# Where two norms' column sums, five transposes and one unread product stand in a matrix engine's stream

## The chip, the cores and the metric

The kernel runs on 1 core of one Trainium2 chip. The metric is the device time in microseconds (us) of that core, the median of the runs shown. TensorE (PE) multiplies, VectorE (DVE), ScalarE (ACT) and GpSimd (POOL) work element by element, SyncE (SP) and GpSimd issue DMAs.

## What is computed

One layer of a hybrid decoder for 256 prompt tokens and 8 x 4 sample tokens with the same weights: an SSD branch and a gated linear attention branch, merged by gates, then cross-attention into 256 memory tokens, then a causal ConvFFN, with an RMS norm ahead of each. Cut to the part that the change touches:

```python
def _rmsnorm(x, g):
    x32 = x.astype(jnp.float32)
    y = x32 * lax.rsqrt(jnp.mean(x32 * x32, axis=-1, keepdims=True) + EPS)
    return (y * g.astype(jnp.float32)).astype(x.dtype)
...
    h = h + _cross_attend(_rmsnorm(h, p['norm_cross']), mem_k, mem_v, p['w_cq'], p['w_co'])

    up = _rmsnorm(h, p['norm_ffn']) @ p['w_up']
    up, ffn_conv_new = _causal_dwconv(up, ffn_conv, p['ffn_conv_w'], p['ffn_conv_b'])
    a, gt = jnp.split(up, 2, axis=-1)
    h = h + (jax.nn.silu(gt) * a) @ p['w_down']
```

D_MODEL is 2048, the ConvFFN is 5632 wide, all data are float32.

## The kernel before

Features lie on the 128 partitions and the 288 tokens (256 + 32) along the free axis, so a projection is `weights^T x activations` with 288 columns. Every projection goes through `proj_w`. It takes two blocks of 128 output columns at a time (a **column pair**, two PSUM accumulators, `j` = 0 and 1) and walks over the input rows in steps of two blocks of 128 (`k`). A weight block is loaded by SP, rounded by ACT to a high part (`whi`, line 103), and DVE takes the remainder as the low part (`wlo`, line 105); five buffers of each let that run ahead of PE. For each step and each `j`, PE does **a six**: four products with the high weights (lines 147 and 148: high and low part of the activations, for two `k`), then two with the low weights (line 151). A column pair over 2048 input rows has 8 steps, so 16 sixes. Sixes, back to back, are most of the program.

The list `late` holds small jobs that are to go into the stream: `proj_w` runs it (`flush`, line 155) behind the third step of a column pair. `tc.block(schedule_with_timeline_sim=True)` lets a scheduler order each engine's instructions by a simulated timeline when the program is built; `tc.keep_in_program_order` pins an instruction against that. What order comes out is shown below from the built program.

Three things in the stretch from the cross-attention to the ConvFFN matter here:

- **The norm's sum.** While the residual `h` is made, its squares are added up in `sqa`. `rstd_of` (line 1394) multiplies `sqa` by a matrix of ones (line 1396, one product of 288 columns in plain float32, where the sixes use the rounded format), which sums over the partitions; ACT then makes the reciprocal root (lines 225 and 226). This is done once for the cross-attention norm (called when the first column pair of `w_cq` is finished, in `q_proj`) and once for the ConvFFN norm (when the first column pair of `w_up` is finished, in `ffn_conv`). The norm is applied to the products' results, so the sixes don't wait for it.
- **The ConvFFN vectors.** Its convolution weights come as rows (`frow`) by DMA and are turned by five transposes on PE (line 1673, `ffn_cols`) into columns `fcol`, between two sixes of the sixth of the eight column pairs of `w_co` (`wo[5]`).
- **The nudge.** `nudge` (lines 119 to 125) puts two transposes of the identity, which nobody reads, behind the third step of the next column pair after the ConvFFN norm's sum.

From there the ConvFFN runs 44 blocks of `w_up` (two halves each) and the products with `w_down`, in sixes alone, to the end of the program.

Of the kernel before, what the change touches and what calls it, by code (L numbers as in the profile page):

```python
# [16 lines left out]
P = 128  # L17
# [6 lines left out]
T = SEQ + NS  # L24
# [18 lines left out]
def hybrid_step(ctx: ExitStack, tc: tile.TileContext, I: dict, O: list):  # L43
# [4 lines left out]
    MM, TR = nc.tensor.matmul, nc.tensor.transpose  # L48
# [12 lines left out]
    def acc_tiles(n):  # L61

        turn[0] += 1
        return [ps.tile([P, 512], F32, tag=f"acc{turn[0] % 2}", bufs=2, name="acc") for _ in range(n)]

    def mm_tile():
        return ps.tile([P, 512], F32, tag="mm", bufs=3, name="mm")

    def la_tile():
        return ps.tile([P, 512], F32, tag="la", bufs=1, name="la")  # L70


    ident = const.tile([P, P], F32, name="ident")
    make_identity(nc, ident)
    ones = const.tile([P, P], F32, name="ones")
# [24 lines left out]
    def wsplit(raw):  # L100

        hi = wp.tile(list(raw.shape), F32R, tag="whi", bufs=WB, name="whi")
        S.copy(hi, raw)  # L103
        lo = wp.tile(list(raw.shape), F32R, tag="wlo", bufs=WB, name="wlo")
        V.tensor_tensor(lo, raw, hi, ALU.subtract)  # L105
        return hi, lo
# [8 lines left out]
        return raw  # L115

    late = []

    def nudge(n):

        def f():
            a = la_tile()
            for _ in range(2):
                tc.keep_in_program_order(TR(a[0:n, 0:P], ident[:, 0:n], ident))
        late.append(f)

    def flush():

        while late:
            late.pop(0)()  # L130

    def proj_w(load, ncol, X, nk, cons, N=T):

        nt = (ncol + P - 1) // P
        accs = acc_tiles(nt)
        for k0 in range(0, nk, 4):
            kn = min(4, nk - k0)
            raw = load(k0, kn)
            for s0 in range(0, kn, 2):
                hi, lo = wsplit(raw[:, s0:s0 + 2, :])  # L140
                for j in range(nt):
                    m = min(P, ncol - j * P)
                    a = accs[j][0:m, 0:N]
                    cs = slice(j * P, j * P + m)
                    for k in range(2):
                        xh, xl = X(k0 + s0 + k)
                        MM(a, hi[:, k, cs], xh, start=(k0 + s0 + k == 0), stop=False)  # L147
                        MM(a, hi[:, k, cs], xl, start=False, stop=False)  # L148
                    for k in range(2):
                        xh, xl = X(k0 + s0 + k)  # L150
                        MM(a, lo[:, k, cs], xh, start=False, stop=(k0 + s0 + k == nk - 1))  # L151
                    if k0 + s0 + 2 == nk:
                        cons(j, a)
                if k0 + s0 == min(4, nk - 2):
                    flush()
                yield
# [7 lines left out]
    def proj(w, c0, ncol, X, nk, cons, row0=0):  # L164
        def load(k0, kn):
            return wload(rows_of(w, row0, k0, kn, c0, ncol))
        return proj_w(load, ncol, X, nk, cons)

    def run(*gens):
        for g in gens:  # L170
            for _ in g:
                pass
# [20 lines left out]
    def split(hi, lo, src):  # L193
        S.copy(hi, src)
        V.tensor_tensor(lo, src, hi, ALU.subtract)
# [27 lines left out]
    def rstd_from(pl, ssq, n, four=False):  # L223
        r = pl.tile([P, T], F32, tag="rstd", bufs=1, name="rstd")
        S.activation(r, ssq, ACT.Ln, scale=1.0 / n, bias=epsc[:, 1:2] if four else epsc[:, 0:1])
        S.activation(r, r, ACT.Exp, scale=-0.5)
        return r
# [1165 lines left out]

    def rstd_of():
        ssq = mm_tile()
        MM(ssq[:, 0:T], ones, rst.pop(), start=True, stop=True)
        return rstd_from(pb, ssq[:, 0:T], D)

    rst = []
    hn = halves(bigr, "hn")  # L1400
    acc = pb.tile([P, T], F32, tag="sqa", bufs=1, name="sqa")
    for j2 in range(KT // 2):
        def cons(j, a, j2=j2):
            added(hx[j2][:, j, :], 2 * j2 + j, a, vec("norm_cross"), hn, acc)
# [18 lines left out]
    def q2(name):  # L1423
        return px.tile([P, 2, 256], F32R, tag="q2", bufs=4, name=name)
# [51 lines left out]
    rc = []  # L1476

    def q_proj(hd):

        qp = []  # L1480
        qps.append(qp)
        for j2 in range(2):
            def cons(j, a, j2=j2):
                if not rc:
                    rc.append(rstd_of())
                if j == 0:
                    qp.append((q2("qh"), q2("ql")))
                d = 2 * j2 + j
                qs = px.tile([P, SEQ], F32, tag="qs", bufs=1, name="qs")
                V.tensor_tensor(qs, a[:, 0:SEQ], rc[0][:, 0:SEQ], ALU.mult)  # L1490
                split(qp[j2][0][:, j, :], qp[j2][1][:, j, :], qs)
                V.tensor_tensor(qsm[:, d], a[:, SEQ:T], rc[0][:, SEQ:T], ALU.mult)
            yield from proj(I["w_cq"], 512 * hd + 256 * j2, 256, hn, KT, cons)
# [126 lines left out]
    def out_cons(j2):  # L1620
        return lambda j, a: added(res["h"][:, 2 * j2 + j, :], 2 * j2 + j, a, vec("norm_ffn"), res["hf"], res["acc"])

    wo = [proj(I["w_co"], 256 * j2, 256, co, KT, out_cons(j2)) for j2 in range(KT // 2)]
    weave(q_proj(0), first_keys(), 16, 16)
    for hd in range(4):
        main = q_proj(hd + 1) if hd < 3 else chain(steps(wo[0], 6), steps(wo[1], 6))
        weave(main, attend(hd), 16 if hd < 3 else 12, 22 if hd else 18)
# [5 lines left out]
    fcol = pf.tile([P, 4, 88], F32, name="fcol")  # L1633
# [43 lines left out]
                V.tensor_copy(gfin, a[:, 0:KT])  # L1677
        carried_turn(0)

    run(*wo[:5])  # L1680
    late.append(ffn_cols)
    run(*wo[5:])
    rst.append(acc)
    rf = []
    store = []

    def ffn_conv(ct, a, out, st, cache):
        if not rf:
            rf.append(rstd_of())
            nudge(P)  # L1690
        u = pf.tile([P, SEQ], F32, tag="fu", bufs=3, name="fu")
        sp = pf.tile([P, NB, 6], F32, tag="fsp", bufs=4, name="fsp")
        G.tensor_copy(sp[:, :, 0:2], st.rearrange("p (b k) -> p b k", k=2))  # L1693
        V.tensor_tensor(u, a[:, 0:SEQ], rf[0][:, 0:SEQ], ALU.mult)
        V.tensor_tensor(sp[:, :, 2:6], a[:, SEQ:T].rearrange("p (b l) -> p b l", l=NL),
                        rf[0][:, SEQ:T].rearrange("p (b l) -> p b l", l=NL), ALU.mult)
        w2, wb = fcol[:, 2, ct:ct + 1], fcol[:, 3, ct:ct + 1]
        S.activation(out[:, 0:SEQ], u, ACT.Identity, scale=w2, bias=wb)
        S.copy(cache[:, 0:2], u[:, SEQ - 2:SEQ])
        S.copy(cache[:, 2:18].rearrange("p (b k) -> p b k", k=2), sp[:, :, 4:6])  # L1700
        outs = out[:, SEQ:T].rearrange("p (b l) -> p b l", l=NL)
        V.tensor_scalar(outs, sp[:, :, 2:6], w2, wb, ALU.mult, ALU.add)
        for k in range(2):
            s = 2 - k
            V.scalar_tensor_tensor(outs, sp[:, :, k:k + 4], fcol[:, k, ct:ct + 1], outs, ALU.mult, ALU.add)  # L1705
            V.scalar_tensor_tensor(out[:, s:SEQ], u[:, 0:SEQ - s], fcol[:, k, ct:ct + 1], out[:, s:SEQ], ALU.mult, ALU.add)
# [17 lines left out]
    def ffn_up(b0, n):  # L1724
        pr = bigr2("pr")
        nb = (b0 + BLK - 1) // BLK
        fst = fsts[nb]
        carried_load(nb + 2)
        carried_turn(nb + 1)
        c = cin[(b0 + BLK - 1) // BLK % 2]  # L1730
        for q0 in range(b0, b0 + n, 4):
            for j2 in range(2):
                av = [pf.tile([P, T], F32, tag="av", bufs=4, name="av") for _ in range(2)]

                def consa(j, a, j2=j2, av=av):
                    t = 2 * j2 + j
                    ffn_conv(q0 + t, a, av[j], fst[:, q0 - b0 + t, 0, :], c[:, 0, q0 - b0 + t, 0:18])

                def consg(j, a, j2=j2, av=av):
                    t = 2 * j2 + j  # L1740
                    gv = pf.tile([P, T], F32, tag="gv", bufs=3, name="gv")
                    ffn_conv(FT + q0 + t, a, gv, fst[:, q0 - b0 + t, 1, :], c[:, 1, q0 - b0 + t, 0:18])
                    S.activation(gv, gv, ACT.Silu)
                    V.tensor_tensor(gv, gv, av[j], ALU.mult)
                    kk = q0 - b0 + t
                    split(pr[:, kk, :], pr[:, BLK + kk, :], gv)
                c0 = (q0 + 2 * j2) * P
                run(proj(I["w_up"], c0, 256, hf, KT, consa))
                run(proj(I["w_up"], FF + c0, 256, hf, KT, consg))
        store.append((b0, n, c))  # L1750
        return pr
# [77 lines left out]
    a = acc_tiles(1)[0]  # L1829
# [62 lines left out]
```

## Time and profile before

| what | us |
| --- | --- |
| three runs | 2503.89, 2500.59, 2503.36 (median 2503.36) |
| the profiled execution, its own time | 2501.66 |
| its span in the trace | 2499.9 |
| PE busy | 2481.9 (99% of the span) |

The span is the time from the first to the last instruction in the trace. Matrix products are pipelined: a product's time in a row runs from its start to its modelled end and overlaps the next one's, so the pace of a stream is read from the starts, or from how many products lie in a stretch, and not from the mean duration.

### The profile page before, as it was taken

To read this page: it belongs to the slowest core of one execution; us is meant where nothing else is said; L and a number is where in the kernel's file an instruction comes from. 1 tells how busy PE (TensorE), PEld (TensorE's weight loads), DVE (VectorE), ACT (ScalarE), POOL (GpSimd) and SP (SyncE) were. 2 spreads that over 40 slices of the span, in tenths; PEclk is the share of its full clock that TensorE was granted. 3 is DMA by queue.
4 is the path that set the end of the run, shared out by engine and by line. 5 is a ranking of instruction groups with operands and counts; after the bars stand their busy time and mean duration, and the time that the engine had idled before them with its cause. 6 is when DMAs were issued, how large, how long until landed. Compare 5 with 4: busy or idle time off the path is not lost.

```text
span 2499.9 us, 50406 instructions
## 1 busy us (share of the span) xinstructions
PE 2481.9 (99%) x18794; PEld 2396.6 (96%) x18794; DVE 1770.6 (71%) x3788; ACT 1332.7 (53%) x2717; POOL 436.1 (17%) x792
## 2 busy tenths in 40 slices
PE   9999999999999999999999999999999999999998
PEld 8889999999999999999999989999999999999998
DVE  6756777787877766776666677667777677675766
ACT  6656547656364655544444545555555454554545
POOL 3102134241311010110111122402111001020012
PEclk9999999999999999999999999999999999999999
DMA  8876687877868686777678699655555555555555
GB/s 254 248 226 197 173 241 223 228 200 213 245 204 298 192 265 193 245 231 237 211 230 272 194 329 328 195 162 173 172 169 172 170 169 173 170 172 169 169 172 169
DMA packets 445302, 528.51 MB, mean 211 GB/s; under 512 B 28492, under 2 KB 391852, under 8 KB 445024
## 3 DMA queue, kind: packets, MB, share of 16 engines
q1 hardware_dynamic: 408512, 422.35, 55.0%
q0 software_dynamic: 36512, 102.93, 13.0%
q8 instruction: 147, 2.41, 0.4%
q14 instruction: 99, 0.81, 0.1%
q10 hardware_dynamic: 32, 0.01, 0.0%
HBM read 476.41 MB, written 48.76 MB: 210 GB/s over the span
## 4 chain that ended last, share of the span: by engine, by line
PE 94%; DVE 2%; DMA 2%; issue 1%; ACT 1%; POOL 0%; DVEq 0%; ACTq 0%; POOLq 0%
PE acc L148 27%; PE acc L147 26%; PE acc L151 26%; PE acc L321 2%; PE acc L322 2%; PE acc L325 2%; DVE wlo L105 1%; PE mm L1187 1%; PE la L1178 1%; PE la L1521 1%; DMA raw<-in_w_co_dram 0%; DMA raw<-in_w_in_dram 0%; PE la L1579 0%; DMA kc<-in_cache_mem_k_dram 0%; PE mm L1151 0%
## 5 line engine op out<-in xcount | busy, mean ns | idle before, releaser
L103 ACT CAST whi<-raw 128x512 fp32r<-128x512 f32 x1464 | 894.3, 618 | 1008.5 <-PE acc L148 731.2
L105 DVE TENSOR_TENSOR wlo<-raw,whi 128x512 fp32r<-128x512 f32 x1464 | 995.1, 687 | 576.6 <-ACT whi L103 563.2
L147 PE MATMUL acc<-xn,whi 128*128 128x288 f32 (+1 forms) x1936 | 543.7, 296 | 0.6 <-DVE sz L652 0.6
L148 PE MATMUL acc<-xn,whi 128*128 128x288 f32 (+1 forms) x1936 | 542.2, 296 | 0.0
L151 PE MATMUL acc<-xn,wlo 128*128 128x288 f32 (+1 forms) x1936 | 409.0, 293 | 0.0
L148 PE MATMUL acc<-hf,whi 128*128 128x288 f32 x1408 | 393.2, 295 | 0.0
L147 PE MATMUL acc<-hf,whi 128*128 128x288 f32 x1408 | 389.0, 292 | 0.0
L147 PEld LDWEIGHTS acc<-xn,whi 128*128 128x128 f32 (+1 forms) x1936 | 364.1, 188 | 8.9 <-issue 4.6
L148 PEld LDWEIGHTS acc<-xn,whi 128*128 128x128 f32 (+1 forms) x1936 | 364.6, 188 | 3.4 <-issue 0.5
L151 PEld LDWEIGHTS acc<-xn,wlo 128*128 128x128 f32 (+1 forms) x1936 | 310.6, 188 | 2.2 <-issue 0.8
L151 PE MATMUL acc<-hf,wlo 128*128 128x288 f32 x1408 | 294.5, 290 | 0.0
L148 PEld LDWEIGHTS acc<-hf,whi 128*128 128x128 f32 x1408 | 264.5, 188 | 0.1
L147 PEld LDWEIGHTS acc<-hf,whi 128*128 128x128 f32 x1408 | 264.0, 188 | 0.1
L151 PEld LDWEIGHTS acc<-hf,wlo 128*128 128x128 f32 x1408 | 226.2, 188 | 0.0
L148 PE MATMUL acc<-pr,whi 128*128 128x288 f32 x704 | 196.6, 295 | 0.0
L147 PE MATMUL acc<-pr,whi 128*128 128x288 f32 x704 | 194.7, 293 | 0.0
L1693 POOL COPY fsp<-fst 128x16 f32<-128x16 f32 x88 | 36.2, 414 | 654.3 <-DVE av L1705 433.2
L151 PE MATMUL acc<-pr,wlo 128*128 128x288 f32 x704 | 147.3, 290 | 0.0
L147 PE MATMUL acc<-un,whi 128*128 128x288 f32 x512 | 143.8, 296 | 0.1
L148 PE MATMUL acc<-un,whi 128*128 128x288 f32 x512 | 143.2, 295 | 0.0
L148 PEld LDWEIGHTS acc<-pr,whi 128*128 128x128 f32 x704 | 132.3, 188 | 0.0
L147 PEld LDWEIGHTS acc<-pr,whi 128*128 128x128 f32 x704 | 132.0, 188 | 0.0
(525 smaller groups left out, 4313.6 us busy)
## 6 DMA issues: line engine op xcount, KB each, us to landing
raw<-in_w_in_dram SPq DMA_DIRECT2D x240, 512.0 KB
raw<-in_w_up_dram SPq DMA_DIRECT2D x176, 512.0 KB
raw<-in_w_down_dram SPq DMA_DIRECT2D x88, 512.0 KB
raw<-in_w_cv_dram SPq DMA_DIRECT2D x32, 512.0 KB
raw<-in_w_ssd_out_dram SPq DMA_DIRECT2D x32, 512.0 KB
sin<-in_state_gla_dram POOLq DMA_DIRECT2D x32, 512.0 KB, 6.1
out_dram<-sin SPq DMA_DIRECT2D x32, 512.0 KB
raw<-in_w_gla_out_dram SPq DMA_DIRECT2D x32, 512.0 KB
```

What stands on the lines that cost most here:

```text
L103: S.copy(hi, raw)
L105: V.tensor_tensor(lo, raw, hi, ALU.subtract)
L147: MM(a, hi[:, k, cs], xh, start=(k0 + s0 + k == 0), stop=False)
L148: MM(a, hi[:, k, cs], xl, start=False, stop=False)
L151: MM(a, lo[:, k, cs], xh, start=False, stop=(k0 + s0 + k == nk - 1))
L321: MM(accs[m], mn_hi[:, kk, ms_], hi[:, 0, :], start=(kk == 0), stop=False)
L322: MM(accs[m], mn_lo[:, kk, ms_], hi[:, 0, :], start=False, stop=False)
L325: MM(accs[m], mn_hi[:, kk, ms_], lo[:, 0, :], start=False, stop=(kk == KT - 1))
L1178: MM(osa[NS * j:NS * j + NS, :], qdm[:, k, b, :], sins[b][:, k, :], start=False, stop=(q == 1 and k == 0))
L1187: MM(a, kb[:, k * P:(k + 1) * P], vst, start=True, stop=True)
L1521: MM(ssc[NS * c:NS * c + NS, 0:P], xq[:, j, u, :], kt[:, j], start=(j == 0), stop=(j == 15))
L1693: G.tensor_copy(sp[:, :, 0:2], st.rearrange("p (b k) -> p b k", k=2))
```

## The change

- `nudge` is gone, with its two transposes.
- A second list `mids` is run by `proj_w` between the high and the low products of a six. Jobs get into it through `late`: a job put into `late` waits for the end of the third step of a column pair, enters `mids` there, and is written into the code in the middle of the fourth step's first six.
- Both norms' sums now go that way, pinned, in the first column pair of `w_cq` and of `w_up`; before, they were written behind that column pair's first finished accumulator.
- `ffn_cols` is put into `late` ahead of `wo[3]` in place of `wo[5]`.
- `guard` is new: a float32 product of `ones` with the first 288 numbers of `fcol`, into the PSUM tile `la`, which nobody reads. It goes through `mids` into `wo[4]`, pinned.

```diff
     late = []
-
-    def nudge(n):
-
-        def f():
-            a = la_tile()
-            for _ in range(2):
-                tc.keep_in_program_order(TR(a[0:n, 0:P], ident[:, 0:n], ident))
-        late.append(f)
-
-    def flush():
-
-        while late:
-            late.pop(0)()
+    mids = []
+
+    def flush(todo=late):
+
+        while todo:
+            todo.pop(0)()
+
+    def guard():
+
+        a = la_tile()
+        tc.keep_in_program_order(MM(a[:, 0:T], ones, fcol.rearrange("p a t -> p (a t)")[:, 0:T], start=True, stop=True))
...
                         MM(a, hi[:, k, cs], xh, start=(k0 + s0 + k == 0), stop=False)
                         MM(a, hi[:, k, cs], xl, start=False, stop=False)
+                    flush(mids)
                     for k in range(2):
...
     def rstd_of():
         ssq = mm_tile()
-        MM(ssq[:, 0:T], ones, rst.pop(), start=True, stop=True)
+        tc.keep_in_program_order(MM(ssq[:, 0:T], ones, rst.pop(), start=True, stop=True))
         return rstd_from(pb, ssq[:, 0:T], D)
...
     def q_proj(hd):
 
+        if not rc:
+            late.append(lambda: mids.append(lambda: rc.append(rstd_of())))
         qp = []
...
             def cons(j, a, j2=j2):
-                if not rc:
-                    rc.append(rstd_of())
...
-    run(*wo[:5])
+    run(*wo[:3])
     late.append(ffn_cols)
-    run(*wo[5:])
+    run(wo[3])
+    late.append(lambda: mids.append(guard))
+    run(*wo[4:])
     rst.append(acc)
     rf = []
+    late.append(lambda: mids.append(lambda: rf.append(rstd_of())))
...
     def ffn_conv(ct, a, out, st, cache):
-        if not rf:
-            rf.append(rstd_of())
-            nudge(P)
```

What the built program has on PE is shown at three places. In these rows `acc` is a column pair's accumulator (two numbers, one for each `j`), `hf0`, `hf1`, `co0` and `co1` the activations, `whi` and `wlo` the weights; the changed file's lines are two or one lower (145, 146, 150 for 147, 148, 151, and 1395 for 1396).

First place, PE, the ConvFFN norm's sum in the first column pair of `w_up`. Before, in the last step:

```order
L151 MATMUL acc_21046<-hf1_19984,wlo_21170 128x288 x2
L1396 MATMUL mm_21178<-sqa_19994,ones_75 128x288
L147 MATMUL acc_21047<-hf1_19984,whi_21168 128x288
L148 MATMUL acc_21047<-hf1_19984,whi_21168 128x288
L147 MATMUL acc_21047<-hf1_19984,whi_21168 128x288
L148 MATMUL acc_21047<-hf1_19984,whi_21168 128x288
L151 MATMUL acc_21047<-hf1_19984,wlo_21170 128x288 x2
```

PE at the same norm in the changed program, in the fourth step:

```order
L145 MATMUL acc_21048<-hf0_19983,whi_21102 128x288
L146 MATMUL acc_21048<-hf0_19983,whi_21102 128x288
L145 MATMUL acc_21048<-hf0_19983,whi_21102 128x288
L146 MATMUL acc_21048<-hf0_19983,whi_21102 128x288
L150 MATMUL acc_21048<-hf0_19983,wlo_21104 128x288 x2
L1395 MATMUL mm_21110<-sqa_19994,ones_75 128x288
L145 MATMUL acc_21049<-hf0_19983,whi_21102 128x288
L146 MATMUL acc_21049<-hf0_19983,whi_21102 128x288
```

The sum moved eight sixes forward, from behind the fifteenth six of the column pair to behind its seventh. In the built order it stands between the sixes of `j` = 0 and `j` = 1, as before, and not inside a six: the two low products, which the code has behind it, come ahead of it. The cross-attention norm's sum in the first column pair of `w_cq` moved in the same way, by the same eight sixes, from a boundary between `j` = 0 and `j` = 1 to another.

Second place, PE, the nudge of before, in the second column pair of `w_up`, between two steps:

```order
L151 MATMUL acc_21216<-hf0_19983,wlo_21255 128x288 x2
L124 MATMUL la_21269<-ident_70 128x128 x2
L147 MATMUL acc_21215<-hf0_19983,whi_21272 128x288
L148 MATMUL acc_21215<-hf0_19983,whi_21272 128x288
L147 MATMUL acc_21215<-hf0_19983,whi_21272 128x288
```

In the changed program the two transposes are not there, and the low products are followed by the next step's first high product at once.

Third place, PE, the transposes of the ConvFFN vectors in the changed program (`wo[3]`, fourth step); before, all five stood in a row between two sixes of `wo[5]`, 32 sixes later:

```order
L150 MATMUL acc_20261<-co0_17475,wlo_20300 128x288 x2
L1672 MATMUL mm_20314<-ident_70,frow_19995 128x128 x2
L145 MATMUL acc_20260<-co0_17475,whi_20325 128x288
L146 MATMUL acc_20260<-co0_17475,whi_20325 128x288
L1672 MATMUL mm_20314<-ident_70,frow_19995 128x128
L145 MATMUL acc_20260<-co0_17475,whi_20325 128x288
L146 MATMUL acc_20260<-co0_17475,whi_20325 128x288
L1672 MATMUL mm_20314<-ident_70,frow_19995 128x128
L150 MATMUL acc_20260<-co0_17475,wlo_20327 128x288 x2
```

The fifth comes in the middle of the next six, again ahead of its low products. The guard, sixteen sixes behind, in the first six of the fourth step of `wo[4]`:

```order
L145 MATMUL acc_20421<-co0_17475,whi_20475 128x288
L146 MATMUL acc_20421<-co0_17475,whi_20475 128x288
L128 MATMUL la_20483<-fcol_19981,ones_75 128x288
L150 MATMUL acc_20421<-co0_17475,wlo_20477 128x288 x2
L145 MATMUL acc_20422<-co0_17475,whi_20475 128x288
```

This one does stand inside its six. On ACT, the two table loads and two activations of each norm (lines 225 and 226) move forward by four casts of weights; on DVE, the copies into `fcol` and the final norm's column move forward by the two column pairs. On POOL and SP nothing moves.

## The prediction

> **What bounds the kernel now.** I read the page's first part and its chain of waits, then PE's waits from the cross-attention on, then the pace of the sixes in stretches, and last PE's timeline around each place that the change touches. The page:
>
> ```profile
> span 2499.9 us, 50406 instructions
> PE 2481.9 (99%) x18794; PEld 2396.6 (96%) x18794; DVE 1770.6 (71%) x3788; ACT 1332.7 (53%) x2717; POOL 436.1 (17%) x792
> PE 94%; DVE 2%; DMA 2%; issue 1%; ACT 1%; POOL 0%; DVEq 0%; ACTq 0%; POOLq 0%
> ```
>
> PE is busy for 99% of the span and makes 94% of the chain. Its waits from 1390 to 2470 us, which is everything between the first norm concerned and the tail:
>
> ```profile
> PE acc L147 <- ACT co L194: 0.9, 1, 0.9
> PE la L1521 <- DVE xqm L1500: 0.4, 1, 0.4
> PE la L1521 <- ACT xqm L1500: 0.3, 1, 0.3
> PE la L1579 <- DMA vc<-in_cache_mem_v_dram: 0.2, 1, 0.2
> ```
>
> These 1.8 us in 1080 all lie in the attention; none is at a norm's sum or at the transposes. So there is no wait here that an earlier sum could remove: PE streams, and what can change is the number of its products and their pace. The pace, from windows that count line 151's products alone (columns: stretch, its length and the products' busy time, their count, granted clock, DMA; two of these products make a six):
>
> ```profile
> 651.25:656.09 4.84, 2.59 (x12) 1.00 0.92 268
> 1159.29:1256.00 96.71, 51.83 (x248) 1.00 0.70 215
> 1291.40:1402.16 110.76, 59.36 (x284) 1.00 0.77 245
> 1404.23:1421.61 17.38, 9.44 (x44) 1.00 0.52 164
> 1582.21:1625.67 43.46, 23.55 (x110) 1.00 0.61 184
> 1627.81:1671.26 43.45, 23.54 (x110) 1.00 0.54 165
> 1673.33:1677.28 3.95, 2.14 (x10) 1.00 0.42 133
> 1679.09:2470.00 790.91, 423.85 (x2028) 1.00 0.56 173
> ```
>
> Length by half the count: 0.807, 0.780, 0.780, 0.790, 0.790, 0.790, 0.790 and 0.780 us for a six. The same six products of 288 columns, at the same granted clock of 1.00, thus run at one of **three paces**, and hold the one they have for as long as nothing else comes between them. The edges are the places of this change. The stretch that ends at 1402 has 0.780, and the cross-attention norm's sum follows; behind it stands 0.790. The stretch up to 1677 has 0.790, and the nudge follows; behind it stand 1014 sixes at 0.780. That last row is the one that matters: 10 ns more for each of them is 10.1 us, and nothing else that the change touches is worth a tenth of that.
>
> [...]
>
> **The change part by part.** The sum is made against the profiled execution: 2501.66 us, its span 2499.9; the median of the runs is 1.7 above that.
>
> *The nudge goes, and what stands around the ConvFFN norm's sum.* PE's timeline at that sum, and at the nudge:
>
> ```profile
> 1671.85 0.65 PE L1396 MATMUL mm<-sqa,ones 128*128 128x288 f32 x2
> ...
> 1673.13 0.29 PE L147 MATMUL acc<-hf,whi 128*128 128x288 f32 x1
> ...
> 1677.87 0.38 PE L124 MATMUL la<-ident 128*128 128x128 f32 x2
> ...
> 1678.89 0.29 PE L147 MATMUL acc<-hf,whi 128*128 128x288 f32 x1
> ```
>
> From 1677.87 to 1678.89 are 1.02 us for the nudge and one six; less 0.79 that makes **-0.23 us**. The sum with its six takes 1.28, so 0.49 of its own, which is paid at the new place as well: 0.
>
> *The pace behind the sum.* This is the term that decides. The first column pair of `w_up` begins 15 sixes before 1671.85, at 1660.0, and the sum's new place, behind seven, is at 1665.5. Up to the nudge's old place lie 15 sixes, which run at 0.790 now. Behind it nothing but sixes comes until the tail's first transposes. If the sum leaves 0.790 behind it as it does now, no nudge ends that: 1015 sixes by 0.010 are **+10.15 us**. Does it? The sum of the other norm, which came out of the faster pace:
>
> ```profile
> 1402.74 0.65 PE L1396 MATMUL mm<-sqa,ones 128*128 128x288 f32 x2
> ...
> 1404.03 0.29 PE L147 MATMUL acc<-hn,whi 128*128 128x288 f32 x1
> ```
>
> It stood between `j` = 0 and `j` = 1 and turned 0.780 into 0.790; the ConvFFN norm's stood at the same kind of place, met 0.790 and left 0.790. In the built order both still stand at just such a boundary. So from either pace the rows say 0.790. The bounds of this term are 0 (pace 0.780) and 1015 x 0.0267 = +27.1 us (pace 0.807).
>
> *The sum inside a six*, which the code asks for and the order doesn't do, has one row of its own kind: another norm's float32 sum of 288 columns at 1157.50, between high and low products.
>
> ```profile
> 1156.98 0.29 PE L147 MATMUL acc<-xn,whi 128*128 128x288 f32 x1
> ...
> 1157.50 0.65 PE L971 MATMUL mm<-sqa,ones 128*128 128x288 f32 x2
> ...
> 1158.26 0.30 PE L147 MATMUL acc<-xn,whi 128*128 128x288 f32 x1
> ...
> 1159.09 0.29 PE L147 MATMUL acc<-xn,whi 128*128 128x288 f32 x1
> ```
>
> Two sixes and the sum take 2.11 us, so its cost is 2.11 - 1.56 = 0.55, and the pace behind it is 0.780 (second row of the windows). The *guard* has this very shape and place: **+0.50 us** (between 0.49 at a boundary and 0.55). What pace it leaves when it meets 0.790 no row shows. The bounds are 0.780 and 0.807 for the 64 sixes between guard and sum (9 of `wo[4]`, 48, 7), -0.64 and +1.07 us; I take the nearest row, L971's, and **-0.64**.
>
> *The five transposes.* Now in a row, and a single one elsewhere in the program:
>
> ```profile
> 1626.26 0.71 PE L1673 MATMUL mm<-ident,frow 128*128 128x128 f32 x5
> ...
> 1627.61 0.29 PE L147 MATMUL acc<-co,whi 128*128 128x288 f32 x1
> ...
> 225.44 0.27 PE L616 MATMUL mm<-ident,cache 128*108 128x128 f32 x1
> ...
> 226.35 0.29 PE L147 MATMUL acc<-xn,whi 128*128 128x288 f32 x1
> ```
>
> Five cost 1.35 - 0.79 = 0.56; a single one 0.91 - 0.78 = 0.13. As a pair (0.23, from the nudge) and three singles they cost 0.62: **+0.06**. The pace of the 16 sixes between them and the guard is open, -0.16 to +0.27 us; I take 0, the pace that they meet. The move takes them 32 x 0.79 = 25.3 us forward, to 1601.0. Their data:
>
> ```profile
> 1587.10 0.52 POOL L1646 DMA_DIRECT2D frow<-in_norm_final_dram  x1
> DMA to landing us min/median/max: 2.3/2.9/3.6
> ```
>
> The last row of `frow` lands by 1590.7, ten microseconds ahead. If that cover were gone, PE would stand still for what is missing, with the whole stream behind it.
>
> *The cross-attention norm's sum* stands 8 sixes earlier, so 8 more run at 0.790 ahead of the attention: **+0.08**. Should it leave another pace, the 150 or so sixes up to the end of the attention could shift with it, by at most -1.5 to +2.5 us; since its place is of the same kind, I take nothing.
>
> *ACT and DVE.* ACT at the ConvFFN norm now, and the last addition into `sqa` on DVE:
>
> ```profile
> 1671.63 1.28 ACT L225 ACT_TABLE_LOAD   x1
> ...
> 1673.95 1.28 ACT L226 ACT_TABLE_LOAD   x1
> ...
> 1677.58 1.14 ACT L103 CAST whi<-raw 128x512 fp32r<-128x512 f32 x2
> 1679.61 0.62 ACT L103 CAST whi<-raw 128x512 fp32r<-128x512 f32 x1 [0.89 <-PE acc L148]
> 1662.42 0.45 DVE L1385 TENSOR_TENSOR sqa<-sqa,sq 128x288 f32<-128x288 f32 x1
> ```
>
> The sum gets a wait on that addition, which ends at 1662.87, 2.6 us ahead of the new place at 1665.5; behind it in PE's queue stand all the sixes, so a later addition would cost its lateness one for one. The table loads push back the casts behind them until 1677.58; two steps later ACT waits for PE again, and PE's waits above show none for `whi`: the five weight buffers hide it, and hide it four casts earlier as well, at 0. Without them it would cost up to the 3.5 us of the two loads and two activations, at each norm. The copies into `fcol` on DVE are as many as before and lie in its idle time between weights.
>
> The sum: -0.23 + 10.15 + 0.50 - 0.64 + 0.06 + 0.08 = **+9.9 us**. On the profiled execution that is 2511.6 us; on the median of 2503.36 it is **2513.3 us**, my forecast.
>
> **The rivals.**
>
> *The sum leaves 0.780* (the other side: not slower). One mechanism, at one place: the guard brings the stream to 0.780, and the ConvFFN norm's sum, met in that state, does not disturb it, so the nudge isn't missed. It decides at the first six behind the sum. For it: a sum inside a six held 0.780 (L971), and the guard is such a product; single foreign products between sixes can hold it too (the transpose at 225.44 is followed by 0.78). Against it: the cross-attention norm's sum lost 0.780 at exactly this kind of boundary. Time: -0.23 + 0.50 + 0.06 + 0.08 - 0.64, and 15 sixes at 0.780 in place of 0.790, -0.15: -0.4 us, so 2503.0.
>
> *The sum leaves 0.807*, the third pace. For it: that pace exists (first row of the windows). Against: neither norm's sum led there. Time: 2503.36 - 0.4 + 27.1, and 15 x 0.027 = 0.4: 2530.5.
>
> *Pace without memory.* One pace for the ConvFFN whatever comes before it; then the tail stays as it is and the change costs its instructions, -0.23 + 0.50 + 0.06: 2503.7. The three paces of the windows speak against it. [...]
>
> *Something else is faster.* From the cross-attention norm to the nudge there are 278 sixes (128 of `w_cq`, 128 of `w_co`, 22 of `w_up`); from 0.790 to 0.780 in all of them is 2.8 us, so a gain of over 0.2% would need a cause that I don't see in the profile.
>
> **How the numbers follow.** Forecast 0.62, the 0.780 rival 0.24, 0.807 0.09, pace without memory 0.03, the rest 0.02. The runs before spread over 3.3 us, and 0.2%, about what a measurement can tell from no change, is 5.0 us. Slower by more than that are the forecast and the 0.807 case, 0.71; within it the 0.780 case and the pace without memory, 0.27; faster 0.02. The forecast's own range is 2511 to 2516 (its open terms and the attention's bounds). The whole range reaches down to the 0.780 case and the attention's gain, 2501, and leaves out the 0.807 case: 2501 to 2516.
>
> **What would show it.** In the profile of the changed kernel: windows over line 150's products (151 now) from 1680 to 2470 us that give 0.790 for a six show the forecast right; 0.780 there makes it wrong by all of 10 us. The windows between guard and sum, 0.780 expected, test the guard; those behind the cross-attention norm's sum, 0.790. The sum itself should cost 0.5 us and the transposes 0.6, and PE's waits should list nothing new at 1601 or 1665. A new wait there for `frow`, `sqa` or `whi` would break the terms that I set to nothing.

## The result, and the profile after

The changed kernel takes **2516.07 us** (median of six runs, 2511.88 to 2520.79). The kernel before takes 2503.72 (six runs, the three above and three more, 2500.59 to 2505.49). The ratio estimated from the runs is 1.0044, with a 95% interval from 1.0035 to 1.0054: 8.8 to 13.5 us slower. (The two medians by themselves lie 12.35 us apart, a ratio of 1.0049.) The forecast was 9.9 us and 2513.3; the measured median lies 0.07 above the top of the range.

The profiled execution took 2516.64 us. The page's first part:

```profile
span 2514.9 us, 50408 instructions
...
PE 2493.0 (99%) x18794; PEld 2406.6 (96%) x18794; DVE 1770.7 (70%) x3788; ACT 1330.4 (53%) x2717; POOL 439.0 (17%) x792
```

PE has the same number of products (two transposes went; the guard, a float32 product, shows as two in the trace) and is busy 11.1 us longer, in a span 15.0 us longer. PE's waits from 1390 to 2485 us:

```profile
PE acc L145 <- ACT co L193: 0.9, 1, 0.9
PE mm L1566 <- ACT prp L1442: 0.4, 1, 0.4
PE la L1520 <- DVE xqm L1499: 0.3, 1, 0.3
```

All three are the attention's again. No wait for `frow`, `sqa`, `fcol` or `whi` has come at any of the places of the change. What remains is the pace. Windows over line 150's products (stretch, its length and the products' busy time, their count, clock, DMA; a six is the length by half the count):

```profile
1404.30:1420.10 15.80, 8.56 (x40) 1.00 0.51 161
1588.20:1605.58 17.38, 9.43 (x44) 1.00 0.65 187
1609.31:1619.58 10.27, 5.57 (x26) 1.00 0.54 160
1621.65:1670.01 48.36, 25.92 (x124) 1.00 0.54 167
1672.86:2484.98 812.12, 440.31 (x2056) 1.00 0.56 170
```

0.790 behind the cross-attention norm's sum, 0.790 ahead of the transposes and behind them, 0.780 from the guard to the ConvFFN norm's sum, and 0.790 from there through 1028 sixes to the tail, where the kernel before had 0.780. The edges, in PE's timeline:

```profile
1606.17 0.38 PE L1672 MATMUL mm<-ident,frow 128*128 128x128 f32 x2
...
1608.32 0.29 PE L145 MATMUL acc<-co,whi 128*128 128x288 f32 x1
...
1619.38 0.29 PE L145 MATMUL acc<-co,whi 128*128 128x288 f32 x1
...
1619.90 0.65 PE L128 MATMUL la<-fcol,ones 128*128 128x288 f32 x2
1620.17 0.65 PE L150 MATMUL acc<-co,wlo 128*128 128x288 f32 x2
1620.66 0.30 PE L145 MATMUL acc<-co,whi 128*128 128x288 f32 x1
...
1670.33 0.42 PE L150 MATMUL acc<-hf,wlo 128*128 128x288 f32 x2
1670.59 0.65 PE L1395 MATMUL mm<-sqa,ones 128*128 128x288 f32 x2
1670.86 0.52 PE L145 MATMUL acc<-hf,whi 128*128 128x288 f32 x1
...
1671.87 0.29 PE L145 MATMUL acc<-hf,whi 128*128 128x288 f32 x1
```

The transposes with two sixes take 2.15, so 0.57 of their own. The guard with its six takes 1.28, so 0.49; it stands between high and low products. The ConvFFN norm's sum with its six takes 1.28, again 0.49; low products stand ahead of it, high ones behind: it stands at a boundary, as in the built order.

The rise of the profiled pair can be split at the sums. From the start of the cross-attention norm's sum to the end are 1097.2 us before (2499.9 - 1402.74) and 1112.9 after (2514.9 - 1402.02). Eight sixes of 0.79 have passed from ahead of that sum to behind it; without these 6.3 us the rise behind it is **9.4 us**. From the start of the ConvFFN norm's sum the same working gives 828.1 and 844.3, less 6.3: **9.9 us**, all of it behind that sum. The remaining 5.6 us of the pair's 15.0 arose ahead of these places, where PE's order in the two programs is the same; the eight sixes themselves, at 0.790 in place of 0.780, are 0.08 of it.

### The profile page after: what moved, and what is told of

The parts are those of the page before. It is cut to its first block, busy times and chain, and to the rows that moved or that the text cites. A ratio compares the mean times of both kernels' runs of the same rounds, so it can differ in the third digit from the quotient of the medians.

```text
span 2514.9 us, 50408 instructions
## 1 busy us (share of the span) xinstructions
PE 2493.0 (99%) x18794; PEld 2406.6 (96%) x18794; DVE 1770.7 (70%) x3788; ACT 1330.4 (53%) x2717; POOL 439.0 (17%) x792
## 4 chain that ended last, share of the span: by engine, by line
PE 88%; issue 5%; DMA 4%; DVE 1%; POOL 1%; ACT 0%; DVEq 0%; POOLq 0%; ACTq 0%
PE acc L146 25%; PE acc L150 25%; PE acc L145 25%; PE acc L320 2%; PE acc L321 2%; PE acc L324 2%; DMA kc<-in_cache_mem_k_dram 1%; DMA sqr<-in_state_ssd_dram 1%; DMA raw<-in_w_cv_dram 1%; PE la L1520 1%; PE la L1177 1%; DMA raw<-in_w_co_dram 1%; PE mm L1186 1%; DMA sin<-in_state_ssd_dram 0%; PE la L1578 0%
## 5 line engine op out<-in xcount | busy, mean ns | idle before, releaser
L150 PE MATMUL acc<-hf,wlo 128*128 128x288 f32 x1408 | 301.5, 295 | 0.0
```

## The experiments

Each comparison is with the kernel before, run on the same chip. A "probe" is a product that nobody reads.

### One part alone, and one part undone

**nudge_out**: the kernel before without its nudge, and nothing else changed.

```diff
             rf.append(rstd_of())
-            nudge(P)
```

> The kernel before with the nudge alone taken out. Theory of the place: a float32 sum between two sixes leaves 0.790 us for a six and nothing but a new disturbance ends it; so 1014 sixes from 1680 us to the tail run at 0.790, +10.15 less the nudge's own 0.23, +9.9 us against the kernel before. Rival of the other edits (guard, spread transposes, earlier sums are what costs, the nudge is ornament): the tail stays at 0.780, -0.2 us. Rival of chance (the pace behind a sum varies from execution to execution): single runs fall apart into two groups 10 us from each other.

Measured: 2516.74 us against 2504.66, ratio 1.0038 [1.0025, 1.0051]. Windows ahead of the ConvFFN norm's sum at 1672.09 and behind it (line 151):

```profile
1628.83:1671.49 42.66, 23.13 (x108) 1.00 0.53 166
1674.35:2469.88 795.53, 431.69 (x2014) 1.00 0.55 169
```

0.790 on both sides, to the tail. This one line brings the whole loss; the earlier sums, the moved transposes and the guard aren't needed for it. The five runs lie within 5.6 us of each other, not in two groups 10 us apart as the rival of chance would have it.

**nudge_back**: the changed kernel with the nudge put back into the next column pair.

```diff
+    nudged = []
     def ffn_conv(ct, a, out, st, cache):
+        if not nudged:
+            nudged.append(1)
+            nudge(P)
```

> The changed kernel with the nudge put back, behind the third step of the second column pair of w_up. Theory of the place: the sixes behind the nudge run at 0.780 again; of the change's cost only 0.5 for the guard, 0.1 for transposes and the earlier first sum less 0.6 for faster sixes behind the guard stay, so 0.0 us against the kernel before, within 0.7. Rival of the other edits: the tail keeps 0.790 and the time stays 10 us above the kernel before.

Measured: 2504.5 us, ratio 0.9999 [0.9991, 1.0007]. The loss is gone. Windows (line 158) ahead of the transposes, behind them, behind the guard, behind the sum, and behind the nudge at 1687.18:

```profile
1592.49:1609.87 17.38, 9.42 (x44) 1.00 0.64 191
1613.64:1623.00 9.36, 5.02 (x24) 1.00 0.55 165
1626.67:1674.25 47.58, 25.54 (x122) 1.00 0.54 166
1677.11:1686.59 9.48, 5.14 (x24) 1.00 0.49 156
1689.17:2469.95 780.78, 418.96 (x2002) 1.00 0.56 172
```

0.790, 0.780, 0.780, 0.790, 0.780. The sum, met at 0.780, leaves 0.790, and the nudge mends it. The second row differs from the changed kernel, where the same transposes in the same order left 0.790; "What else changes the pace" below comes back to this.

### The place of the sum

**sums_inside**: the changed kernel, still without a nudge, with `mids` held back by one step. In the code the sums stay in the middle of a six; one step later the built order keeps them there.

```diff
-                    flush(mids)
+                    if k0 + s0 >= 8:
+                        flush(mids)
```

> The changed kernel with the middle jobs run one step later (from the fifth step of a column pair on), by which the built order has both sums and the guard between the high and the low products of a six; no nudge. Theory of the place: a sum inside a six leaves 0.780, so the whole ConvFFN runs at 0.780 without a nudge: -0.2 nudge, +0.5 guard, +0.1 for two sums at 0.55, +0.1 transposes, -0.6 behind the guard, -0.2 up to where the nudge stood, -0.3 between the first sum and the attention: -0.6 us against the kernel before. Rival (what was missing is the nudge, wherever the sum stands): the tail runs at 0.790, +10 us.

Measured: 2504.35 us, ratio 0.9998 [0.9988, 1.0008]. PE's timeline at the ConvFFN norm's sum, and windows (line 151) behind the cross-attention norm's sum, between guard and ConvFFN sum, and behind the latter:

```profile
1669.69 0.29 PE L146 MATMUL acc<-hf,whi 128*128 128x288 f32 x1
1669.83 0.65 PE L1396 MATMUL mm<-sqa,ones 128*128 128x288 f32 x2
1670.10 0.65 PE L151 MATMUL acc<-hf,wlo 128*128 128x288 f32 x2
```

```profile
1402.33:1417.93 15.60, 8.36 (x40) 1.00 0.49 153
1621.92:1668.72 46.80, 25.11 (x120) 1.00 0.52 165
1672.39:2467.99 795.60, 426.89 (x2040) 1.00 0.56 172
```

0.780 in all three. The same sums, with the same waits and readers, some sixes later and between high and low products, don't lower the pace.

**inside_no_guard**: the same without the line that puts the guard into `wo[4]`.

```diff
-    late.append(lambda: mids.append(guard))
```

> As the run with the sums inside their sixes, without the guard, so the ConvFFN norm's sum meets whatever pace the transposes leave (0.790 in the changed kernel). If a float32 product inside a six sets 0.780 whatever it meets, as the guard did when it met 0.790, the tail runs at 0.780: against the run with the guard -0.5 for the guard and +0.7 for the 72 sixes ahead of the sum, so +0.2, and -0.4 us against the kernel before. If it only keeps the pace that it meets, the tail runs at 0.790: +10 us.

Measured: 2503.96 us, ratio 0.9995 [0.9983, 1.0006]. Windows (line 151) from the transposes to the ConvFFN norm's sum and behind it:

```profile
1602.93:1662.99 60.06, 32.23 (x154) 1.00 0.55 169
1666.66:2464.60 797.94, 428.20 (x2046) 1.00 0.56 172
```

In this execution the transposes left 0.780 by themselves, so the sum didn't meet 0.790 and the question whether it would raise the pace on its own stayed open.

**one_inside** asks that question with the transposes where the kernel before has them: no nudge, the cross-attention norm's sum as before, and the ConvFFN norm's alone inside a six.

```diff
+                    if k0 + s0 >= 8:
+                        flush(mids)
...
+    late.append(lambda: mids.append(lambda: rf.append(rstd_of())))
...
-        if not rf:
-            rf.append(rstd_of())
-            nudge(P)
```

> The kernel before without its nudge, with the ConvFFN norm's sum alone inside a six; the cross-attention norm's sum and the five transposes stay where the kernel before has them. The stream should meet the sum at 0.790. Theory of the place, in its strong form: a float32 product inside a six sets 0.780, so the sum itself does the nudge's work: 0.780 to the tail, 0.4 us under the kernel before. Weak form (inside a six the pace is only kept): 0.790 stays, about 10 us over the kernel before.

Measured: 2505.84 us against 2505.92, ratio 0.9996 [0.9987, 1.0005]. Windows (line 154) ahead of the sum at 1665.29 and behind it:

```profile
1627.05:1664.17 37.12, 20.14 (x94) 1.00 0.53 164
1667.04:2464.97 797.93, 427.61 (x2046) 1.00 0.57 172
```

0.790 ahead, 0.780 behind. The strong form holds: a sum between high and low products not only keeps the faster pace, it sets it.

### A product in place of a norm

Four kernels add to the kernel before, nudge and all, an unread product of the guard's kind, behind the nudge where 0.780 stands. It brings no norm's table loads, no wait on a late addition, and no reader.

**probe_steps**, between two steps of the third column pair:

```diff
+    def probe():
+        a = la_tile()
+        tc.keep_in_program_order(MM(a[:, 0:T], ones, fcol.rearrange("p a t -> p (a t)")[:, 0:T], start=True, stop=True))
...
+        calls.append(1)
+        if len(calls) == 3:
+            late.append(probe)
```

> The kernel before, nudge and all, with one more unread float32 product of 288 columns in the ConvFFN's third column pair, between two steps (behind the low products of j = 1, ahead of the high ones of j = 0). Theory of the place: a float32 product between sixes leaves 0.790 us a six whatever it is for, so all sixes from the probe to the tail's first transposes (about 1000) go from 0.780 to 0.790; with 0.5 us for the probe itself about 10.5 us over the kernel before, near 2514.5. Rival, the norm and not the product (the waits, table loads and readers that come with a norm's sum lower the pace): the probe has none of these, the pace stays 0.780, and the cost is 0.5 us.

Measured: 2517.37 us against 2505.92, ratio 1.0046 [1.0034, 1.0059]. Windows (line 153) ahead of the probe at 1695.09 and behind it:

```profile
1684.37:1694.51 10.14, 5.43 (x26) 1.00 0.57 178
1697.37:2479.47 782.10, 424.06 (x1980) 1.00 0.56 170
```

**probe_between**, the same product between `j` = 0 and `j` = 1 in the last step of the second column pair (`between` is one more list of jobs, like `mids`):

```diff
                     if k0 + s0 + 2 == nk:
                         cons(j, a)
+                    if j == 0:
+                        flush(between)
...
+            between.append(probe)
```

> The same probe at the other kind of boundary, between the sixes of j = 0 and j = 1 of the last step of the second column pair, where the norms' sums stand. Theory of the place: 0.790 behind it, about 10.5 us over the kernel before. Rival, only the boundary between two steps (or only a norm's sum) lowers the pace: 0.780, 0.5 us.

Measured: 2517.3 us, ratio 1.0041 [1.0027, 1.0055]. Behind the probe at 1690.49 (line 153):

```profile
1692.77:2479.61 786.84, 426.72 (x1992) 1.00 0.56 170
```

**probe_inside**, the same product four products further on in the stream, inside the six of `j` = 1:

```diff
                         MM(a, hi[:, k, cs], xl, start=False, stop=False)
+                    flush(mids)
...
+            mids.append(probe)
```

> The same probe six products later or earlier, inside a six (between its high and its low products). Theory of the place: 0.780 is kept, cost 0.55 us, no difference to the kernel before that the times can tell. Rival, any foreign float32 product lowers the pace: about 10.5 us over the kernel before.

Measured: 2505.28 us, ratio 1.0003 [0.9994, 1.0013]. The probe in PE's timeline, and the window behind it (line 153):

```profile
1687.55 0.29 PE L149 MATMUL acc<-hf,whi 128*128 128x288 f32 x1
1687.68 0.65 PE L1694 MATMUL la<-fcol,ones 128*128 128x288 f32 x2
1687.95 0.65 PE L153 MATMUL acc<-hf,wlo 128*128 128x288 f32 x2
```

```profile
1689.47:2469.47 780.00, 418.00 (x2000) 1.00 0.57 172
```

0.790 behind the two probes at boundaries, 0.780 behind the one inside. A bare product does at each place what the norm's sum does there; the rival that put the pace down to the norm falls.

### Which gap of the six

Is it that the accumulator is the same on both sides of the foreign product, or the step from high to low weights? Two more probes stand in other gaps of a six.

**probe_p2**, behind the second high product (this diff and the next are against probe_inside):

```diff
                         MM(a, hi[:, k, cs], xl, start=False, stop=False)
-                    flush(mids)
+                        if k == 0:
+                            flush(mids)
```

> The kernel before with the unread float32 product inside a six of the second column pair, but behind the second high product in place of behind the fourth. If what counts is that the products ahead and behind add into the same accumulator, 0.780 is kept (0.55 us, same time as before). If what counts is the step from high to low weights, this place need not keep it: 0.790 (+10.5 us) or 0.807 (+27 us).

Measured: 2506.23 us against 2505.82, ratio 1.0002 [0.999, 1.0014]. Behind the probe (line 154):

```profile
1695.06:2475.06 780.00, 418.07 (x2000) 1.00 0.57 172
```

**probe_p5**, between the two low products:

```diff
-                    flush(mids)
...
                         MM(a, lo[:, k, cs], xh, start=False, stop=(k0 + s0 + k == nk - 1))
+                        if k == 0:
+                            flush(mids)
```

> The same, between the two low products of the six. Same accumulator on both sides: 0.780 by the first theory. By the rival (high to low counts) 0.790 or 0.807, +10.5 or +27 us.

Measured: 2516.96 us, ratio 1.004 [1.0027, 1.0053]. The probe in the timeline, and the window behind it (line 152):

```profile
1694.18 0.29 PE L152 MATMUL acc<-hf,wlo 128*128 128x288 f32 x1
1694.31 0.65 PE L1695 MATMUL la<-fcol,ones 128*128 128x288 f32 x2
1694.58 0.51 PE L152 MATMUL acc<-hf,wlo 128*128 128x288 f32 x1
```

```profile
1696.72:2485.14 788.42, 427.41 (x1996) 1.00 0.56 170
```

0.780 behind the first, 0.790 behind the second, which has the same accumulator on both sides. So both simple rules fall. What stands is a map: a float32 product of 288 columns leaves 0.780 in the gap behind two or behind four products of a six, and 0.790 in the gap behind five and at the boundary. The gaps behind one and three weren't tried.

**probe_twice**: the product at the boundary of probe_steps, and once more three sixes later, behind the second high product of a six. The code asks for both at the boundary; it is the built order that puts the second one there.

```diff
         if len(calls) == 3:
             late.append(probe)
+            late.append(probe)
```

> The unread float32 product twice in the third column pair: first between two steps (0.790 behind it, as that probe alone showed), then three sixes later behind the second high product of a six. If a product inside a six sets 0.780 whatever it meets and whichever gap of the six it is in, 0.780 from there to the tail and 1.0 us over the kernel before. If only the gap between high and low products resets it, 0.790 and about 11 us over.

Measured: 2507.03 us, ratio 1.0005 [0.9994, 1.0015]. Windows (line 153) ahead of the first probe, between the two, and behind the second:

```profile
1683.86:1694.00 10.14, 5.43 (x26) 1.00 0.59 177
1696.86:1697.65 0.79, 0.43 (x2) 1.00 0.52 106
1699.71:2469.56 769.85, 412.57 (x1974) 1.00 0.56 172
```

0.780, 0.790, 0.780: within one execution the same instruction lowers the pace in one gap and restores it in another, three sixes later.

**nudge_one**: one transpose in the nudge in place of two.

```diff
-            for _ in range(2):
+            for _ in range(1):
```

> The kernel before with one unread transpose in the nudge in place of two, between the same two steps. If any transposes at a boundary set 0.780, the time is that of the kernel before less 0.1 us. If the number matters (two undo what one does), 0.790 stays to the tail: about 10 us over.

Measured: 2516.03 us, ratio 1.004 [1.0027, 1.0053]. The window behind the single transpose at 1678.05 (line 151):

```profile
1679.94:2474.68 794.74, 430.93 (x2012) 1.00 0.56 170
```

0.790: one transpose at that boundary doesn't lift the pace, two do. That a foreign product stands there isn't enough.

**What else changes the pace.** The kept traces show two things that limit the map.

First, in eight of the 14 profiled kernels the pace changes between 1165 and 1400 us, where PE runs nothing but sixes. Each time a product comes late there. In probe_p2 two low products wait for their weights; ahead of them and behind them stand (line 154):

```profile
1263.97 0.53 PE L154 MATMUL acc<-xn,wlo 128*128 128x288 f32 x2 [1.61 <-DVE wlo L105]
```

```profile
1183.90:1261.90 78.00, 41.80 (x200) 1.00 0.70 214
1265.40:1344.40 79.00, 42.80 (x200) 1.00 0.79 256
```

That is 0.780 and 0.790, with no foreign product. In probe_steps the two low products at 1364.8 us come 7 ns late together, and 0.790 follows 0.780; in nudge_back a low product comes 43 ns late at 1345.0, and 0.780 follows 0.790. Not every late product does it: in the changed kernel a wait of 0.7 us at 1262.9 leaves 0.780 as it was. So a foreign product seems to be one disturbance among others. From 1705 to 2465 us no product of any of the 14 kernels comes more than 15 ns late, and there each keeps the pace that it had.

Second, 0.790 has two states. By the starts in the trace every six at 0.780 is like the next, but at 0.790 two forms take turns: in the changed kernel's ConvFFN the fourth high product follows the third by 130.8 ns in one and by 127.5 in the other. The six ahead of the spread transposes had the second form in the changed kernel and in sums_inside, which left 0.790, and the first in nudge_back and inside_no_guard, which left 0.780. So the same order can give either pace, by the state that it meets; four executions are too few to call this shown. A sum at a boundary left 0.790 from both forms. The products inside a six and the nudges that lifted 0.790 each met only one form at their gap.

Every kernel was profiled once, so a pace is seen in one execution of each. The medians fit it; single runs overlap (the lowest with 0.790 is 2511.36 us, the highest of a kernel with 0.780 is 2513.36).

## Why the prediction was right, step by step

**The deciding term**, +10.15 us for the pace behind the ConvFFN norm's sum, was right: 0.790 through the ConvFFN, 9.9 us from that sum to the end with the -0.23 of the nudge in it. The step behind it was right too: not the code, which asks for the middle of a six, but the built order, which puts the sum at a boundary. sums_inside shows it from the other side: with the sum truly inside, the loss isn't there. Why the scheduler keeps the job inside one step later and not at the fourth step wasn't looked into.

**The guard**: 0.49 against the 0.50 taken. Its pace came out at 0.780, and the -0.64 for the sixes up to the sum with it. The one row behind this choice had met 0.780 and the guard met 0.790, so that was in part luck; one_inside showed it again.

**The transposes**: 0.57 against 0.62. The 16 sixes behind them ran at 0.790, the value taken; other executions of the same order left 0.780 there (nudge_back, inside_no_guard), so that it held here was luck, and the term stays open by about 0.2 us.

**The cross-attention norm's sum** left 0.790, as taken. The stretch between the two sums gives 0.5 us less than before (269.1 and 268.6), where the terms said 0.1 less; such a difference lies within the bound given for the attention.

**What was set to nothing** stayed nothing: no new wait at the sums, the transposes or the guard.

**The rival that the sum leaves 0.780** was right that the guard brings 0.780 to the sum; it failed at the sum, which turned 0.780 into 0.790 at its boundary. sums_inside shows the end that it described, in an order that the change doesn't have. 0.807 stood behind no sum. **The pace without memory** falls with every pair above: probe_between and probe_inside differ by four places in the order and by 12 us. The Trainium skill ("TensorE: Matmul & The Clock Gate", section "Back-to-back issue gap") gives, for a stream of weight loads and products, one measured spacing for each of two widths, about 81 ns at 128 columns and 131 ns at 512. No run here has these widths in a stream; at 288 columns and a granted clock of 1.00 the same product has two spacings here, 130.0 and 131.7 ns (0.780 and 0.790 by six).

**That a pace holds until something else comes between the sixes** was too strong as a general statement. It held from the sum to the tail, which is all that the forecast needed; between 1165 and 1400 us the pace also changed behind late products. The prediction's count of 278 sixes at 0.790, in its last rival, has 15 of `w_cq` that ran at 0.780 (2.6 us in place of 2.8), which changes nothing.

**The size.** Measured were 12.35 us between the medians, interval 8.8 to 13.5, where the sum said 9.9. In the profiled pair the excess lies ahead of the change. The old norm's sum, in the middle of a six at 1157.50 before, comes 4.4 us later after. The two longest of PE's waits up to there, of after and then of before:

```profile
PE mm L902 <- ACT cst L617: 2.9, 1, 2.9
PE mm L615 <- DVE sin L905: 2.3, 1, 2.3
```

```profile
PE mm L903 <- ACT cst L618: 1.6, 1, 1.6
PE mm L616 <- DVE sin L906: 1.4, 1, 1.4
```

They are the same two waits, for ACT's `cst` and DVE's `sin`, and 2.2 us longer in one execution than in the other; another 1.6 us had arisen by 50 us. That is spread and not the change: over the 14 profiled kernels, all of which share the order up to this place, the same sum starts between 1154.98 (one_inside) and 1164.32 us (nudge_back). So a single pair of profiles can carry 9 us that have nothing to do with an edit made at 1400 us; what this pair shows of the change is what the stretches behind the edit show, 9.4 to 9.9. For the other runs, which have no profile, that the rest of the 12.35 is spread too is not shown, but the interval, 8.8 to 13.5, holds 9.9. The six kernels that end in 0.790 give 1.0038 to 1.0046, about 9.5 to 11.5 us.

No version tried beats the kernel before: those that hold 0.780 to the tail have ratios from 0.9995 to 1.0005.

## What to carry to other kernels

When one engine streams for most of the span, read its pace per repeated group, stretch by stretch, and look for the small instructions at which it changes: 10 ns in 780 over a thousand groups outweighed everything else here, and no table of waits shows it. What decides for an inserted product is its place in the order that was built, not the line in the code, so read the built order ahead of trusting an edit that is about place. The state in which the stream meets it may count as well, and behind a weight that came late the pace changed as well. Measure an edit from the first place that it touches, since what lies ahead of it may vary by more than the edit is worth.

## What the runs showed of the hardware

- Six products of 288 columns with their weight loads run in a stream at 0.780 or 0.790 us, at a granted clock of 1.00. Undisturbed, they keep that pace over a thousand repetitions (all 14 profiles from 1705 to 2465 us). A foreign product can change it, and it also changed behind products that came late (probe_p2 at 1264 us, 0.780 to 0.790).
- A float32 product of 288 columns costs 0.5 us by itself. In which gap of the six it stands sets the pace that follows. Behind two products (probe_p2, probe_twice) or four (probe_inside, one_inside, the guard) that is 0.780, and at a boundary (the sums, probe_steps, probe_between) 0.790, from either pace; behind five (probe_p5) it is 0.790, tried from 0.780 alone. These are single profiled executions.
- Two transposes at a boundary lift 0.790 to 0.780, one doesn't. Five spread over two sixes left 0.790 in two executions and 0.780 in two others, in the same order; the two pairs differ in the form of the six ahead of them.
- Why the gap decides is open. The spacing of the products within a six differs between the two paces; it repeats from six to six at 0.780 and every second six at 0.790. No run here shows which part of PE holds it.
